# A second output buffer for the experts of a hybrid encoder layer, and one load buffer fewer

## The chip, the cores and the metric

The kernel runs on one core of one Trainium2 chip. The metric is the time of one execution on the device in microseconds (us), as the median of several runs. The engines are named as in the profile: PE (TensorE matmul), PEld (its weight loads), DVE (VectorE), ACT (ScalarE), POOL (GpSimd) and SP (SyncE). SP only issues transfers here; POOL issues the transfers that need an index per row.

## The reference

One layer of an encoder for 512 tokens of 1024 values, in float32. A first part (differential attention beside a gated linear recurrence, merged and projected) is not touched by the change. The last part is a mixture of experts:

```python
h2 = rms_norm(x, norm2_gain)
# router: one group of 4 by softmax and argmax, then 2 of its 4 experts; weights cs
a = einsum('nd,edf->nef', h2, w_gate)       # 16 experts, 1024 -> 512
u = einsum('nd,edf->nef', h2, w_up)
hid = silu(a) * u * cs[:, :, None]
y = einsum('nef,efd->nd', hid, w_down)      # 512 -> 1024, summed over the experts
x = x + y
```

Each token uses 2 of the 16 experts.

## The kernel before

The layer is computed in stages; the last one, from about 610 us on, is the experts' (lines 961 to 1094). The experts run one after the other. An expert has 104 slots for tokens. Its tokens are fetched by row index from DRAM (the "gather", L882) into one of two places of the buffer `hy`, transposed on PE (`xgp`) and split into exact high and low parts (`hx`). The products with the gate, up and down weights are each done as three PE passes (L1027 to L1029) over the weights' high and low parts.

The weights come in 12 loads of 512 KB for each expert (four of gate, four of up, four of down), 192 in all. Each load lands in one of 33 buffers that are used in turn (the list `raws`, with names such as `mr`, `raw`, `u0`, `h2`); a buffer comes free when ACT has copied its load to the high part (L171, `we_h` or `wd_h`) and DVE has formed the low part (L172, `we_l` or `wd_l`). All but three loads are issued by SP in one fixed order (L974); loads number 31 to 33, the first into the buffers `h2`, `h2` and `g2`, are issued by POOL (L972). The high and low parts have four buffers each.

The order of the program in one turn of the loop (expert e) is: gate product of e; in its middle the transposes of the hidden values of e - 1 (`hpt`, L1001); down product of e - 1 into two PSUM tiles `py`, with the transposes of the tokens of e + 1 and the slot search of e + 3 between its four loads; then the output of e - 1: two ACT copies of `py` (104x512 each, L1058) into a place of `hy`, and one transfer that adds the 104 rows to `out` in DRAM by index (the "scatter", L886, issued by POOL); then the up product of e. The framework orders instructions on each engine once, when the kernel is built, by an estimate of their readiness. So ACT, POOL and SP each work through a fixed list, and an instruction that waits holds up everything behind it on its engine.

The output has one place, `place(hy, 1, 0)`. The copies of expert e write where the scatter of expert e - 1 reads, so the first copy waits until that scatter has landed. Below, copy n, scatter n and gather n are those of expert n, counted from 0; gather n + 4 stands in POOL's list next to scatter n.

```python
add_out(ids[e][0].ix, py, place(hy, 1, 0)[0:CAP])     # end of down(e), L1053

def add_out(ix, py, y):
    for n in range(2):
        ACT.copy(y[:, n * 512:(n + 1) * 512], py[n])
    scatter_add(ix, y)
```

Of the kernel before, what the change touches and what calls it, by code (L numbers as in the profile page):

```python
# [10 lines left out]
F32 = mybir.dt.float32  # L11
# [8 lines left out]
P = 128  # L20
D = 1024
S = 512
# [11 lines left out]
RAW1 = 9  # L34
# [4 lines left out]
BEHIND = 30  # L39
# [7 lines left out]
# columns of the per-partition parameter block  # L47
# [7 lines left out]
# columns of the row parameters that every partition needs  # L55
# [6 lines left out]
# columns of the constants  # L62
# [45 lines left out]
def hybrid_layer(ctx, tc, x, w_in, w_ao, w_lo, w_out, w_lg, w_rt, w_eg, w_eu, w_ed, pp, rw, cst, out):  # L108
# [45 lines left out]
    # places of 4 KB, with one use after the other: tag -> (pool, number)  # L154
# [19 lines left out]
    def load_split(src, name, behind=()):  # L174
        # one chunk [128, 8, 256] of dense weights, in two halves of its rows
        hs, ls_ = [], []
        for i in range(2):
            t = wraw.tile([P, 1024], F32, tag="raw", name=f"{name}_r{i}")
            nc.sync.dma_start(t, src[:, i * 1024:(i + 1) * 1024])
            hi = wspl.tile([P, 1024], F32R, tag="whi", name=f"{name}_h{i}")  # L180
            lo = wspl.tile([P, 1024], F32R, tag="wlo", name=f"{name}_l{i}")
            with ExitStack() as order:
                for ins in behind[i:i + 1]:
                    order.enter_context(tc.issue_after(ins))
                split(hi, lo, t)
            hs += [hi[:, q * 256:(q + 1) * 256] for q in range(4)]
            ls_ += [lo[:, q * 256:(q + 1) * 256] for q in range(4)]
        return hs, ls_

    def mm3(ps, wh, wl, ah, al, first=True, last=True):  # L190
        # stationary (wh, wl), moving (ah, al)
        mm(ps, wh, ah, start=first, stop=False)  # L192
        mm(ps, wh, al, start=False, stop=False)  # L193
        return mm(ps, wl, ah, start=False, stop=last)

# [36 lines left out]
    # softplus(-lam) = max(-lam, 0) + log1p(exp(-|lam|)); log1p(z) = 2 atanh(z / (2 + z))  # L232
# [23 lines left out]
    # lambda of the differential attention, on every partition  # L256
# [9 lines left out]
    # rotary tables with the gains (k's carry sqrt(64))  # L266
# [20 lines left out]
    held = []          # what waits for results of the tensor engine, with how much of its next work goes before it  # L287
# [4 lines left out]
    def go_on(last, n):  # L292
        # n columns have passed up to here
        for h in held:
            h[0] -= n
        due = [h for h in held if h[0] <= 0]
        for h in due:
            held.remove(h)
            with tc.issue_after(last.ins):
                h[1]()  # L300
# [16 lines left out]
    gat = tc.alloc_tile_pool(name="gat", bufs=1)  # L317
    gT = gat.tile([P, KD, S], F32, name="gT")          # tanh of the lru gate, then the gated lru branch
# [7 lines left out]
    yG = [yp.tile([P, 2, S], F32, tag=f"y{j}", name=f"yG{j}") for j in range(4)]      # gelu(lru_gate)  # L326
    yT = [[None] * 4, [None] * 4]                                                     # the branch's output takes its place
    lp = tc.alloc_tile_pool(name="lru", bufs=1, side="right", reuse_waits="tile")
    xpt = [lp.tile([P, S + 3], F32, name=f"xp{i}") for i in range(2)]      # with the convolution's margins
# [5 lines left out]
    def gate_pieces(i, dst):  # L335
        # columns of gate_attn (i < 4) or gate_lru
        w = []

        def piece(cb):
            if cb == 0:  # L340
                w.extend(load_split(w_in[20 + i], f"wg{i}"))
            j = 2 * i + cb
            ps = pj(f"gps{j}")
            proj_T(ps, w, cb, h_)
            ACT.activation(dst[:, j % 8], ps, AF.Tanh, bias=hb[:, 32 + j:33 + j], scale=0.5)

        return [lambda: piece(0), lambda: piece(1)]
# [111 lines left out]
    def qk_half(pr, qi, tp):  # L459
        # half of the tokens of q (k) of two heads: projected and rotated; sums of squares for its norm  # L460
# [44 lines left out]
    def stack(pr, hh, qi):  # L505
        # transposed, then exact parts on top of each other: q as [hi; lo], k as [hi; lo] and [lo; hi]
        # (of the head's second map the other way round)
        j = pr.j
        ps = pm(f"tps{qi}{j}{hh}")
        for t in range(NT):  # L510
            PE.transpose(ps[:, t * P:(t + 1) * P], pr.qr[qi][:, t, hh * P:(hh + 1) * P], ident)
        names = ("q",) if qi == 0 else ("k0", "k1")
        st = [unit(n, [P, 2, S], F32R, f"st_{n}{j}{hh}") for n in names]
        for s in range(2):
            own, oth = slice(64 * s, 64 * s + 64), slice(64 - 64 * s, 128 - 64 * s)
            a = st[0][:, s]
            ACT.copy(a[own], ps[own])
            DVE.tensor_tensor(a[oth], ps[own], f(a[own]), op=ALU.subtract)
            pr.st[hh, qi, s, 0] = a
            if qi:  # L520
                b = st[1][:, s]
                ACT.copy(b[oth], ps[own])
                DVE.tensor_copy(b[own], a[oth])
                pr.st[hh, qi, s, 1] = b
# [24 lines left out]
    def apply_v(pr, hh, t, mx, ee):  # L549
        # e0 - lam (s0 / s1) e1, times v: the head's output times s0  # L550
# [50 lines left out]
    def new_o(h):  # L601
        # exact parts of a head's output, where the last heads' operands have left room
        o = unit(("qr", "qr", "va", "vb", "q", "k0", "k1", "ee")[h], [P, 2, S], F32R, f"o{h}")
        oS[h] = o[:, 0], o[:, 1]
        return oS[h]
# [8 lines left out]
    # lru branch projected and gated: gT <- (1 + tanh) * lru_d; the first two heads beside it  # L614
# [8 lines left out]
    # for the second norm and the router: the gains carry sqrt(D); the router takes x2 itself, the gain in its weights  # L623
# [25 lines left out]
    # what runs beside each step of a pair of heads: projections of the next pair, operands, gates  # L649
# [50 lines left out]
    places["sq"] = mraw1, 1  # L700
    x2 = [unit(tag, [P, D], F32, f"x2_{tag}") for tag in ("u0", "u1", "u2", "rope")]
# [23 lines left out]
    # of each token and expert, for its slot: valid, token in two parts, zero, weight and 1 / rms in three parts  # L725
# [4 lines left out]
    def post(t, part, c0, c1, then, eng=None):  # L730
        # of some columns: sum of squares, and the router's products with x2 turned
# [22 lines left out]
    def scaled(eng, t, c0, c1):  # L754
        # part of the normed tokens but for 1 / rms; written in two halves of the columns
        i = t // 2, c0 // 512
        if c0 % 512 == 0 and t % 2 == 0:
            h2[i] = unit("h2", [P, 2, 512], F32, f"h2_{t}{c0}")
        half = h2[i][:, t % 2]
        i_ = eng.tensor_tensor(half[:, c0 % 512:(c1 - 1) % 512 + 1], x2[t][:, c0:c1], g2r[:, c0:c1], op=ALU.mult)  # L760
        if c1 % 512 == 0:
            nc.sync.dma_start(h2d[t * P:(t + 1) * P, c1 - 512:c1], half)
        return i_.ins
# [22 lines left out]
    # group and experts of each token; its places within the experts, from 1; 0 where not chosen  # L786
# [3 lines left out]
    def route(t):  # L790
        # how many of the groups (of the group's experts) go before each one: larger, or equal and of a lower index
# [14 lines left out]
        # the tokens before those of the next block; the last time, all of them  # L806
# [8 lines left out]
    class Slots:  # L815
        # token (or a spare row), weight and 1 / rms of each slot of expert e, ranks CAP r ...
# [22 lines left out]
        def ids(self):  # L839
            # id = p + 128 t + (1 - valid) * slot  # L840
# [48 lines left out]
    # the tokens and their outputs lie where the merged branches were  # L889
# [7 lines left out]
    ids = {}  # L897

# [18 lines left out]
    # combine weights (with 1 / rms of the token), as exact bf16 parts  # L917
# [79 lines left out]
    def turn(name, src, k0, dst):  # L997
        # four blocks of 128 columns, transposed: [CAP, 4, 128] -> [128, 4, CAP], copied or split
# [26 lines left out]
    def mm3_(ps, ah, al, wh, wl, first, last):  # L1025
        # stationary (ah, al), moving (wh, wl)
        mm(ps, ah, wh, start=first, stop=False)  # L1027
        mm(ps, ah, wl, start=False, stop=False)  # L1028
        mm(ps, al, wh, start=False, stop=last)  # L1029
# [10 lines left out]
    def down(e, ht, between):  # L1040
# [12 lines left out]
        add_out(ids[e][0].ix, py, place(hy, 1, 0)[0:CAP])  # L1053
# [145 lines left out]
```

## Time and profile before

| | |
|---|---|
| median of 3 timed runs | 934.54 us (934.34 to 935.6) |
| profiled execution, first to last instruction (span) | 937.4 us |
| PE busy | 881.9 us, 94% of the span |
| DVE / ACT / POOL busy | 699.8 / 588.3 / 212.4 us |
| moved by the transfer engines | 169.99 MB, mean 181 GB/s |

The page gives no other time of the profiled execution than its span, which is 2.9 us above the median of the timed runs; differences are therefore worked out within the profiled execution and taken off the median. An engine's busy share is an average over the stages, so each stage is read from its own stretch of time.

### The profile page before, as it was taken

The numbers are of one execution on the slowest core, as the hardware profiler recorded it, in microseconds if no ns is written. First come the engines' busy times: TensorE is split into PE (matmuls) and PEld (weight loads), VectorE is DVE, ScalarE is ACT, GpSimd is POOL, SyncE is SP. The second block draws the span as 40 slices with busy tenths as digits, with TensorE's granted clock in tenths as the row PEclk, the third lists the DMA queues.
The fourth block names the chain that finished last, engine by engine and source line by source line (L and its number), as shares of the span: only waits on it lengthen the run. The fifth ranks groups of instructions, "written<-read, shape, count | busy, mean of one in ns | idle before, by whom it ended". The sixth has DMA issues, their size and how long they took to land. (4 is left out here: it accounts for less than half of the span.)

```text
span 937.4 us, 13453 instructions
## 1 busy us (share of the span) xinstructions
PE 881.9 (94%) x4950; PEld 729.2 (78%) x4950; DVE 699.8 (75%) x1077; ACT 588.3 (63%) x917; POOL 212.4 (23%) x183
## 2 busy tenths in 40 slices
PE   4999999999999999999999999877999999999993
PEld 3887787889999889999888899855676777777772
DVE  4548978854488688896895643676897999999992
ACT  6698796622364664664785323345786888888881
POOL 6500000053026026053110003331442131121010
PEclk9999999999999999999999999978999999999998
DMA  6421312232212112112226286689999999999922
GB/s 229 171 72 63 138 68 91 96 133 90 90 62 75 50 58 71 49 46 68 105 98 234 103 296 227 218 296 259 334 375 334 375 375 355 349 377 352 376 60 36
DMA packets 48061, 169.99 MB, mean 181 GB/s; under 512 B 6177, under 2 KB 6225, under 8 KB 47985
## 3 DMA queue, kind: packets, MB, share of 16 engines
q1 hardware_dynamic: 41040, 147.34, 43.3%
q0 software_dynamic: 6944, 21.68, 9.0%
q8 instruction: 41, 0.67, 0.3%
q14 instruction: 36, 0.29, 0.1%
HBM read 156.94 MB, written 12.06 MB: 180 GB/s over the span
## 5 line engine op out<-in xcount | busy, mean ns | idle before, releaser
L172 DVE TENSOR_TENSOR we_l<-we,we_h 128x1024 fp32r<-128x1024 f32 x128 | 153.8, 1224 | 21.7 <-ACT we_h L171 19.8
L171 ACT CAST we_h<-we 128x1024 fp32r<-128x1024 f32 x128 | 132.1, 1051 | 25.7 <-PE mgu L1029 14.1
L1027 PE MATMUL mgu<-we_h,hx 128*104 128x512 f32 x256 | 103.6, 405 | 3.1 <-ACT we_h L171 2.5
L1028 PE MATMUL mgu<-we_l,hx 128*104 128x512 f32 x256 | 103.1, 403 | 1.7 <-DVE we_l L172 1.6
L1029 PE MATMUL mgu<-we_h,hx 128*104 128x512 f32 x256 | 102.5, 400 | 0.0
L171 ACT CAST wd_h<-wd 128x1024 fp32r<-128x1024 f32 x64 | 67.3, 1051 | 24.1 <-PE mgu L1029 24.1
L167 POOL TENSOR_TENSOR rk<-ss,mhalf 128x8 f32<-128x8 f32 x16 | 26.4, 1648 | 245.6 <-DVE ss L474 245.6
L172 DVE TENSOR_TENSOR wd_l<-wd,wd_h 128x1024 fp32r<-128x1024 f32 x64 | 77.6, 1222 | 5.8 <-ACT wd_h L171 5.7
L886 POOL DMA_INDIRECT out_dram<-hy,ix x16 | 33.4, 2090 | 191.8 <-DVE ix L844 112.6
L312 PE MATMUL qps<-wqk_l,hT 128*128 128x256 f32 x256 | 72.4, 283 | 1.2 <-DVE wqk_l L172 1.2
L311 PE MATMUL qps<-wqk_h,hT 128*128 128x256 f32 x256 | 73.4, 287 | 0.0
L313 PE MATMUL qps<-wqk_h,hT 128*128 128x256 f32 x256 | 72.5, 283 | 0.0
L1027 PEld LDWEIGHTS mgu<-we_h,hx 128*104 128x104 f32 x256 | 44.0, 172 | 19.8 <-ACT we_h L171 3.4
L1028 PEld LDWEIGHTS mgu<-we_l,hx 128*104 128x104 f32 x256 | 44.0, 172 | 18.3 <-DVE we_l L172 2.7
L1029 PEld LDWEIGHTS mgu<-we_h,hx 128*104 128x104 f32 x256 | 44.1, 172 | 16.0
L545 ACT ACTIVATE ee<-sps,mx 128x512 f32<-128x512 f32 x64 | 43.9, 691 | 17.1 <-DVE mx L544 17.0
L544 DVE TENSOR_REDUCE mx<-sps 128x1 f32<-128x512 f32 x64 | 42.6, 682 | 16.1 <-PE sps L542 15.9
L1027 PE MATMUL py<-wd_h,hh 128*104 128x512 f32 x128 | 52.5, 414 | 0.6 <-ACT hh L171 0.6
L192 PE MATMUL gps<-hT,wg_h 128*128 128x512 f32 x128 | 50.8, 397 | 0.0
L1029 PE MATMUL py<-wd_h,hl 128*104 128x512 f32 x128 | 50.4, 395 | 0.0
L1028 PE MATMUL py<-wd_l,hh 128*104 128x512 f32 x128 | 50.3, 393 | 0.0
L193 PE MATMUL gps<-hT,wg_h 128*128 128x512 f32 x128 | 50.3, 393 | 0.0
(307 smaller groups left out, 2535.0 us busy)
## 6 DMA issues: line engine op xcount, KB each, us to landing
wd<-in_w_ed_dram SPq DMA_DIRECT2D x64, 512.0 KB, 12.4
we<-in_w_eg_dram SPq DMA_DIRECT2D x63, 512.0 KB, 12.9
we<-in_w_eu_dram SPq DMA_DIRECT2D x62, 512.0 KB, 11.6
wg_r<-in_w_in_dram SPq DMA_DIRECT2D x16, 512.0 KB, 3.6
wqk_r<-in_w_in_dram SPq DMA_DIRECT2D x16, 512.0 KB, 3.6
wy_r<-in_w_in_dram SPq DMA_DIRECT2D x8, 512.0 KB, 5.5
wx_r<-in_w_in_dram SPq DMA_DIRECT2D x8, 512.0 KB
wlo_r<-in_w_lo_dram SPq DMA_DIRECT2D x8, 512.0 KB, 4.1
```

What stands on the lines that cost most here:

```text
L171: ACT.copy(dst_hi, src)
L172: eng.tensor_tensor(dst_lo, src, f(dst_hi), op=ALU.subtract)
L192: mm(ps, wh, ah, start=first, stop=False)
L193: mm(ps, wh, al, start=False, stop=False)
L311: mm(ps, a, w[0][k], start=(k == 0), stop=False)
L312: mm(ps, a, w[1][k], start=False, stop=False)
L313: last = mm(ps, b, w[0][k], start=False, stop=(k == KD - 1))
L544: DVE.tensor_reduce(mx[:, c:c + 1], ps, axis=AX.X, op=ALU.max, negate=True)
L545: ACT.activation(ee[:, c], ps, AF.Exp, bias=mx[:, c:c + 1], accum_out=(pr.s0s[hh][:, t:t + 1] if c == 0 else mx[:, 3:4]))
L1027: mm(ps, ah, wh, start=first, stop=False)
L1028: mm(ps, ah, wl, start=False, stop=False)
L1029: mm(ps, al, wh, start=False, stop=last)
```

## The change

A new buffer `y2` of [128, 1024] float32 is allocated in the pool in which the load buffers named `mr` lie. The copies and the scatter of experts with an odd number use `y2`, those with an even number use the place in `hy` as before. To make room, the buffers named `mr` are five instead of six (`RAW1 - 3`), so that the list `raws` has 32 entries instead of 33, and `BEHIND` goes from 30 to 29, so that the last three loads of the first round (now number 30 to 32, again into `h2`, `h2` and `g2`) are still the ones that POOL issues. The new file also has no comments, and its lines stand one lower from line 700 on and two lower from line 900 on.

```diff
-RAW1 = 9
+RAW1 = 8
...
-BEHIND = 30
+BEHIND = 29
...
     places["mr"] = mraw1, RAW1 - 3
     places["h2"] = mraw1, 2
     places["sq"] = mraw1, 1
+    places["y2"] = mraw1, 1
...
     ids = {}
+    y2 = unit("y2", [P, D], F32, "y2")
...
-        add_out(ids[e][0].ix, py, place(hy, 1, 0)[0:CAP])
+        add_out(ids[e][0].ix, py, (y2 if e % 2 else place(hy, 1, 0))[0:CAP])
```

ACT's list around the output of expert 1, before. A name in brackets is a semaphore that the instruction waits for; DMASW ones tell of the landing of a transfer that POOL issued, DMAHW ones of one that SP issued. Copy 1 is the first row with `COPY`.

```order
L171 CAST we_h<-we_6570 128x1024 [waits DMASW4_49,DVE_49,PE_49]
L1058 COPY hy<-py_6465 104x512 [waits DMASW2_49,PE_49]
L1058 COPY hy<-py_6466 104x512 [waits PE_49]
L171 CAST we_h<-we_6582 128x1024 [waits DMASW5_49,DVE_49]
L171 CAST we_h<-we_6599 128x1024 [waits DVE_49,DMASW6_49,PE_49,Activation_49]
```

The same place of ACT's list now:

```order
L171 CAST we_h<-we_6571 128x1024 [waits DMASW5_49,DVE_49,PE_49]
L1060 COPY y_5989<-py_6466 104x512 [waits PE_49]
L1060 COPY y_5989<-py_6467 104x512 [waits PE_49]
L171 CAST we_h<-we_6583 128x1024 [waits DMASW6_49,DVE_49]
L171 CAST we_h<-we_6600 128x1024 [waits DVE_49,PE_49,Activation_49]
```

The order is the same; copy 1 no longer waits for DMASW2, which scatter 0 raises.

POOL's list there now (L883 is a gather, L887 a scatter; ix0 to ix7 are the experts' indices). It has the same order as before, with `hy_5988` in place of `y2_5989`:

```order
L883 DMA hy_5988<-h2d_238,ix4_0_6334 104x1024 [waits DMASW7_49,DVE_49,PE_49]
L887 DMA out_0_dram<-hy_5988,ix0_0_5982 640x1024 [waits DMASW3_49,Activation_49]
L887 DMA out_0_dram<-y2_5989,ix1_0_5999 640x1024 [waits DMASW2_49,Activation_49]
L883 DMA hy_5988<-h2d_238,ix5_0_6523 104x1024 [waits DMASW0_49,DMASW4_49,DVE_49,PE_49]
L883 DMA hy_5988<-h2d_238,ix6_0_6712 104x1024 [waits DMASW1_49,DMASW5_49,DVE_49,PE_49]
L887 DMA out_0_dram<-hy_5988,ix2_0_6072 640x1024 [waits DMASW6_49,DMASW3_49,Activation_49]
L887 DMA out_0_dram<-y2_5989,ix3_0_6190 640x1024 [waits DMASW6_49,Activation_49]
```

What each scatter waits for is unchanged: scatter 1 still waits for DMASW2, the landing of scatter 0. SP's list is the old one with each load of the experts one buffer further on.

## Rows read from the trace of the kernel before

**Rows 1.** Busy time by stretch: PE, PEld, DVE, ACT, POOL, granted clock, DMA share, GB/s.

```profile
740.00:760.00 20.00, 20.00 (x100) 14.81 (x99) 19.19 (x22) 16.88 (x21) 3.63 (x2) 1.00 1.03 360
```

**Rows 2.** Waits of PE, 640 us on: total, times, longest (us).

```profile
PE mgu L1027 <- ACT we_h L171: 2.5, 2, 1.3
PE mgu L1028 <- DVE we_l L172: 1.6, 2, 0.8
```

**Rows 3.** Timeline of PE (start, length, idle before, releaser): the first waits.

```profile
676.38 0.47 PE L1027 MATMUL mgu<-we_h,hx 128*104 128x512 f32 x1 [1.13 <-ACT we_h L171]
...
715.03 0.47 PE L1027 MATMUL mgu<-we_h,hx 128*104 128x512 f32 x1 [1.34 <-ACT we_h L171]
```

**Rows 4.** Timeline of ACT: copies 1, 2 and 3.

```profile
674.31 1.07 ACT L1058 COPY hy<-py 104x512 f32<-104x512 f32 x2 [3.75 <-DMA out_dram<-hy,ix]
...
690.87 1.26 ACT L1058 COPY hy<-py 104x512 f32<-104x512 f32 x2
...
712.96 1.07 ACT L1058 COPY hy<-py 104x512 f32<-104x512 f32 x2 [3.98 <-DMA out_dram<-hy,ix]
```

**Rows 5.** Waits of ACT, 640 us on.

```profile
ACT hy L1058 <- DMA out_dram<-hy,ix: 7.7, 2, 4.0
```

**Rows 6.** Timeline of POOL, 653 to 718 us: scatters L886, gathers L882.

```profile
659.98 4.44 POOL L886 DMA_INDIRECT out_dram<-hy,ix  x1 [0.30 <-ACT we_h L171]
675.69 1.62 POOL L886 DMA_INDIRECT out_dram<-hy,ix  x1 [11.27 <-ACT hy L1058]
677.62 2.00 POOL L882 DMA_INDIRECT hy<-h2d,ix  x1 [0.30 <-DVE we_l L172]
693.27 6.21 POOL L882 DMA_INDIRECT hy<-h2d,ix  x1 [13.65 <-PE mgu L1029]
699.78 4.40 POOL L886 DMA_INDIRECT out_dram<-hy,ix  x1 [0.30 <-ACT wd_h L171]
714.34 1.62 POOL L886 DMA_INDIRECT out_dram<-hy,ix  x1 [10.16 <-ACT hy L1058]
```

**Rows 7.** Timeline of PE: hpt of experts 1 to 5; xgp of expert 5.

```profile
661.32 0.52 PE L1001 MATMUL hpt<-cst_sb,hy 104*128 104x104 f32 x4
...
681.66 0.52 PE L1001 MATMUL hpt<-cst_sb,hy 104*128 104x104 f32 x4
...
699.65 0.52 PE L1001 MATMUL hpt<-cst_sb,hy 104*128 104x104 f32 x4
...
704.24 0.52 PE L1001 MATMUL xgp<-cst_sb,hy 104*128 104x104 f32 x4
...
721.87 0.52 PE L1001 MATMUL hpt<-cst_sb,hy 104*128 104x104 f32 x4
...
739.83 0.52 PE L1001 MATMUL hpt<-cst_sb,hy 104*128 104x104 f32 x4
```

**Rows 8.** Busy time by stretch, around the second wait of PE.

```profile
716.90:720.30 3.40, 3.40 (x10) 2.31 (x9) 3.40 (x5) 1.96 (x2) 1.36 (x1) 0.50 1.05 364
720.30:730.00 9.70, 9.70 (x53) 7.24 (x52) 8.73 (x9) 8.00 (x10) 0.00 (x0) 1.00 1.03 352
```

**Rows 9.** Transfer issues: queue, count, KB each, median us to landing.

```profile
wd<-in_w_ed_dram SPq DMA_DIRECT2D x64, 512.0 KB, 12.4
...
hy<-h2d,ix POOLq DMA_INDIRECT x16, 11.2
```

**Rows 10.** Timeline of SP: issues of four loads each.

```profile
649.65 6.13 SPq L974 DMA_DIRECT2D wd<-in_w_ed_dram  x4
...
879.68 6.48 SPq L974 DMA_DIRECT2D wd<-in_w_ed_dram  x4
```

**Rows 11.** Timeline of ACT: the cast of the last load.

```profile
915.56 1.05 ACT L171 CAST wd_h<-wd 128x1024 fp32r<-128x1024 f32 x1 [0.31 <-PE mgu L1029]
```

**Rows 12.** Busy time by stretch: where loads wait for buffers, and the last full one.

```profile
650.00:656.00 6.00, 5.91 (x29) 4.07 (x28) 4.40 (x7) 4.96 (x7) 2.04 (x1) 1.00 0.63 227
...
880.00:890.00 10.00, 10.00 (x53) 7.44 (x51) 9.37 (x10) 8.22 (x11) 0.00 (x0) 1.00 1.03 372
```

## The prediction

> **What bounds the kernel now.** I read the stage of the experts first by its busy time per stretch. In a full stretch of 20 us PE is busy for all 20, DVE for 19.19 and ACT for 16.88, and the transfer engines' share is 1.03 [rows 1]. So PE sets the pace, and the loads run at the engines' limit beside it. The view of waits, from 640 us to the end, says how often PE is held up there: twice by a high part from ACT, 2.5 us in all, and twice by a low part from DVE, 1.6 us in all [rows 2]; two waits further on, in the last expert, come after the last load was cast and are not touched. PE's timeline puts the two pairs at 676 and at 715 us [rows 3].
>
> Going back one step, ACT's timeline shows what held the high parts up. Copy 1 begins at 674.31 after ACT stood idle for 3.75 us, and copy 3 at 712.96 after 3.98 us, both released by the landing of a scatter; copy 2, between them, did not wait [rows 4]. These two are all the time that copies lost to scatters, 7.7 us in 2 waits [rows 5]. Back one more step, POOL's timeline: scatter 0 starts only at 659.98, right behind a gather, and takes 4.44 us to issue; scatter 2 starts at 699.78, behind a gather of 6.21 us, and takes 4.40 us; scatters 1 and 3 take 1.62 us each [rows 6]. From their starts to the release of the copies, scatter 0 needs 674.31 - 659.98 = 14.3 us and scatter 2 needs 712.96 - 699.78 = 13.2 us. So the single place for the outputs binds at two experts of sixteen, where the scatter started late.
>
> **What the two waits cost.** What an expert takes without a wait is read from the distance of the transposes hpt: from expert 2 to 3 it is 699.65 - 681.66 = 17.99 us, and from 4 to 5 it is 739.83 - 721.87 = 17.96 us; I take 17.98. From 1 to 2 it is 681.66 - 661.32 = 20.34 us, and from 3 to 4 it is 721.87 - 699.65 = 22.22 us [rows 7]. The waits therefore cost 2.36 and 4.24 us. Of the second, 3.40 us passed at a granted clock of 0.50 (1.2 instead of 2.4 GHz) after PE had stood still, from 716.90 on; at full clock the same work takes half, so 1.70 us are the clock's [rows 8]. The rest is PE's idle time, (2.5 + 1.6) = 4.1 us in both places [rows 2], and some 0.8 us of slow start.
>
> **What the change removes.** Copy 1 writes `y2`, which nobody has read yet, and in ACT's list it has no wait for a transfer left. Copy 2 waits for scatter 0, copy 3 for scatter 1, and so on: one turn more. With PE 2.36 us ahead, copy 2 comes at 690.87 - 2.36 = 688.5 [rows 4], and scatter 0 landed at 674.3, 14 us before. Scatter 1 can start when scatter 0 has landed, at 674.3, and by the slowest of the two landings, 14.3 us, it is through at 688.6; copy 3 comes at 712.96 - 3.98 - 2.36 = 706.6, 18 us after. Both waits of ACT go, with nothing in their place on ACT: 2.36 + 4.24 = 6.60 us.
>
> **What the change adds.** No instruction: the same 32 copies and 16 scatters, of the same shapes. Two costs remain to be bounded.
>
> First, POOL. Scatter 1 still waits for scatter 0, and what is queued behind it is gather 5, then gather 6. Gather 5 started at 677.62 [rows 6]; now it starts behind scatter 1 at about 674.3 + 1.62 + 0.3 = 676.2. It lands a median of 11.2 us later [rows 9], at 687.4, and PE wants it for the transposes xgp of expert 5, which stood at 704.24 [rows 7] and come 2.36 us earlier: 14 us of cover. In the same way scatter 3 waits for scatter 2, which lands 13.2 us after its start at 699.78 - 2.36, so at 710.6; gather 7 follows at about 712.5 and lands at 724, and expert 7's transposes come a whole turn after 721.87 - 6.60. The cost is 0; without the cover PE would wait for the gather as it would for any operand, by what exceeds those 14 us.
>
> Second, the ring of 32 buffers. A load now waits until the next load in the order has been consumed, one step longer. That matters where the loads already wait for buffers: from 650 to 656 us the transfer share is only 0.63 [rows 12], and four loads were issued over 6.13 us, so (6.13 - 0.33) / 3 = 1.93 us apart, the 0.33 being one issue [rows 10]. There everything lands about 1.9 us later, and since the engines are full from then on (share 1.03 up to 890 us [rows 1, 12]) it stays so. What hides it is the lead of the loads: the last is issued at 879.68 + 6.48 = 886.2 at the latest [rows 10], lands by the median of 12.4 us [rows 9] at 898.6, and is cast at 915.56 [rows 11], so the lead is 17.0 us. It falls to 17.0 - 6.6 - 1.9 = 8.5 us and stays positive. Cost 0; if the cover were gone, PE would lose what is missing from it.
>
> The sum: 0 - 6.60 + 0 + 0 = -6.60 us. In the profiled execution this is 937.4 - 6.6 = 930.8 us of span; I take the same difference off the median of the timed runs, 934.54 - 6.60 = 927.94, because the waits' causes (an order and its durations) are no different there. The unknown is how much of the loss PE gets back. At the least it is the idle time alone, 4.1 us (930.4): ACT and DVE could stay as close behind as they are now, and the clock could fall elsewhere. At the most it is all that ACT lost, 7.7 us [rows 5], and the clock's 1.70, so 9.4 us (925.1). I take the distances between the transposes, since they measure PE's own loss whole.
>
> Of the clock, the Trainium skill (TensorE: Matmul & The Clock Gate, Part 1) says that how many slow matmuls a kernel meets varies from run to run of the same kernel. The trace has one execution, so no run here shows that yet; by that rule the 1.70 us would be missing in some runs before, and the gain there would be 4.90 us.
>
> **The rivals.** *A part only comes back:* PE gains the idle time and no more, 4.1 us, 930.4. For it: the clock at 0.50 is seen after one of the two waits only, so it need not be bound to them. Against it: the distances 17.99 and 17.96 on either side show what a turn without a wait takes.
>
> *The wait moves to POOL:* the scatters still go one at a time, so POOL stands where ACT stood, and the gathers behind are late. It decides once a gather loses its 14 us of cover, so with landings of 28 us instead of 14; if the gathers of experts 5 and 7 were late by what was won, 2.36 and 4.24, the time would stay at 934.5. For it: POOL's list, in which scatter 1 waits for DMASW2 as before. Against it: the landings are 14.3 and 13.2 us, under the 17.98 of a turn, so the chain of scatters does not fall behind.
> The Trainium skill (DMA: Bandwidth & Descriptors, Rules for kernel authors) speaks for this rival: a transfer that accumulates must wait for an earlier one to the same bytes, since a write in between is lost. By that rule a second buffer never puts two scatters in flight, and what it frees is ACT alone; the order of the new kernel agrees.
>
> *The shorter ring starves PE (slower):* if the loads, with 32 buffers, kept waiting for buffers as between 650 and 656 us, they would come 1.93 us apart, while PE uses one each 17.98 / 12 = 1.50 us. The lead would shrink by 0.43 us per load; the 8.5 us that are left are gone after 20 loads, the 6.6 us gained after 15 more. Over 50 loads, four experts, PE would lose 50 x 0.43 - 8.5 = 13.0 us, and the time would be 934.54 - 6.60 + 13.0 = 940.9. For it: one stretch with the share at 0.63, and a buffer less. Against it: the share is full in every later stretch that I read, and buffers come free earlier once PE no longer stands.
>
> *It does not do what it says:* the even copies could still be held because `hy` also holds tokens and hidden values. The order excludes it for copy 1, and copy 2 did not wait before either; I give it no chance of its own beyond the second rival's.
>
> **How the numbers follow.** The forecast, both waits gone, has 0.76 (927.9; its own range 925.1 to 930.4); a part only 0.11 (930.4); moved to POOL 0.08 (934.5); starved 0.05 (940.9). A measurement of this kernel tells 0.2%, 1.9 us, from no change. The first two cases are faster: 0.87, of which I leave 0.01 to a gain under 1.9 us; same 0.09; slower 0.05, so faster 0.86. The range takes the forecast's own bounds and 1 us beyond the partial case for the lead that I only know by a median: 925.0 to 931.5.
>
> **What would show it.** Right: in the profile after, no copy released by a scatter; PE's waits for high and low parts gone between 660 and 730 us; all distances of hpt from expert 1 to 12 near 17.98; the granted clock 1.00 through 700 to 730 us; the last load's cast still well after its landing. POOL should show scatters 1 and 3 waiting for the scatters before them, with no wait of PE for tokens. Wrong: distances over 18.5 us with a copy or a gather as releaser (second rival), or PE behind high parts that wait for loads (third). A gain under 4 us with all waits gone would mean that the distances measured something else than these waits.

## The result and the profile after

Over 16 runs each, the changed kernel has a median of 930.53 us (927.79 to 933.28) and the kernel before one of 935.93 us (932.88 to 939.75). The ratio is 0.9933, with a 95% interval of 0.9921 to 0.9946. Of 935.93 us that is 6.3 us less, between 5.1 and 7.4; the medians alone differ by 5.4 us. The forecast was 6.60 us less, and 927.9 us in all; the time came out 2.6 us higher, 1.4 us of which is the median of before, which stood at 934.54 us in the three runs shown then.

The waits of PE from 640 us on (total, times, longest, in us) are now these. The pairs of [rows 2] are gone; the two that are left belong to the last expert and were there before.

```profile
PE hpt L1003 <- DVE hy L1039: 0.8, 1, 0.8
PE py L1029 <- ACT hh L171: 0.6, 1, 0.6
```

ACT's timeline of the changed kernel (start, length in us), copies 1, 2 and 3, which answer to [rows 4]. None has an idle time and a releaser in brackets behind it any more.

```profile
668.40 1.25 ACT L1060 COPY y<-py 104x512 f32<-104x512 f32 x2
...
686.39 1.27 ACT L1060 COPY hy<-py 104x512 f32<-104x512 f32 x2
...
704.35 1.25 ACT L1060 COPY y<-py 104x512 f32<-104x512 f32 x2
```

PE's timeline, the transposes hpt of experts 0 to 5 and of 15:

```profile
633.72 0.52 PE L1003 MATMUL hpt<-cst_sb,hy 104*128 104x104 f32 x4
...
659.25 0.52 PE L1003 MATMUL hpt<-cst_sb,hy 104*128 104x104 f32 x4
...
677.19 0.52 PE L1003 MATMUL hpt<-cst_sb,hy 104*128 104x104 f32 x4
...
695.18 0.52 PE L1003 MATMUL hpt<-cst_sb,hy 104*128 104x104 f32 x4
...
713.14 0.52 PE L1003 MATMUL hpt<-cst_sb,hy 104*128 104x104 f32 x4
...
731.13 0.52 PE L1003 MATMUL hpt<-cst_sb,hy 104*128 104x104 f32 x4
...
907.70 0.58 PE L1003 MATMUL hpt<-cst_sb,hy 104*128 104x104 f32 x4 [0.84 <-DVE hy L1039]
```

And the same of before for experts 0 and 15; expert 1's is in [rows 7].

```profile
634.31 0.52 PE L1001 MATMUL hpt<-cst_sb,hy 104*128 104x104 f32 x4
...
916.36 0.57 PE L1001 MATMUL hpt<-cst_sb,hy 104*128 104x104 f32 x4 [0.84 <-DVE hy L1037]
```

From expert 1 to 15 it took 916.36 - 661.32 = 255.04 us before, and takes 907.70 - 659.25 = 248.45 us now: 6.59 us less. Up to expert 12 every turn (from one hpt to the next) now takes 17.94 to 18.00 us; before, two took 20.34 and 22.22. The last three turns are shorter in both kernels (17.76, 17.74 and 15.23 us now). This distance is used below for every kernel ("1 to 15"), because it leaves out what happens ahead of expert 1.

That stretch ahead matters for one reading. The profiled span fell by 937.4 - 928.9 = 8.5 us, more than the 6.59. Most of the rest, 27.01 - 25.53 = 1.48 us, lies between expert 0 and 1. Busy time by stretch, of before and then of after (the columns as in [rows 1]; the last but two is the granted clock):

```profile
638.40:641.80 3.40, 2.25 (x10) 2.03 (x11) 0.99 (x2) 1.01 (x2) 0.00 (x0) 0.50 1.03 317
641.80:645.20 3.40, 3.40 (x9) 2.32 (x8) 0.74 (x1) 1.04 (x1) 0.00 (x0) 0.50 1.05 236
```

```profile
638.40:641.80 3.40, 3.12 (x13) 2.62 (x14) 0.59 (x1) 1.01 (x2) 0.00 (x0) 0.50 1.05 289
641.80:645.20 3.40, 3.40 (x16) 2.52 (x15) 1.85 (x3) 2.10 (x2) 0.00 (x0) 1.00 1.00 264
```

The clock stood at 0.50 in both halves before and in the first half only after. A second profile of the changed kernel (after2, below) has 0.50 and 0.54 there, and 27.08 us from expert 0 to 1. So this part varies between executions of one kernel, and the change has no claim on it.

POOL's timeline after, from gather 4 on, answers to [rows 6]:

```profile
651.90 5.72 POOL L883 DMA_INDIRECT hy<-h2d,ix  x1 [15.57 <-DVE ix L845]
657.93 4.44 POOL L887 DMA_INDIRECT out_dram<-hy,ix  x1 [0.30 <-ACT we_h L171]
672.74 1.74 POOL L887 DMA_INDIRECT out_dram<-y,ix  x1 [10.38 <-DMA out_dram<-hy,ix]
674.79 4.87 POOL L883 DMA_INDIRECT hy<-h2d,ix  x1 [0.30 <-DVE M L832]
688.12 5.05 POOL L883 DMA_INDIRECT hy<-h2d,ix  x1 [8.45 <-issue]
693.48 1.63 POOL L887 DMA_INDIRECT out_dram<-hy,ix  x1 [0.30 <-issue]
706.23 1.70 POOL L887 DMA_INDIRECT out_dram<-y,ix  x1 [11.13 <-DVE ix L845]
```

Scatter 1 now waits on POOL for scatter 0. But something changed that the prediction had not foreseen: gather 6 and scatter 2 take 5.05 + 1.63 = 6.7 us to issue, where they took 6.21 + 4.40 = 10.6 us. So scatter 2 is out early, and scatter 3 needs no wait for it.

### The profile page after: what moved, and what is told of

Read it like the earlier page. It is cut to its first block, busy times and chain, and to the rows that moved or that the text cites. A ratio compares the mean times of both kernels' runs of the same rounds, so it can differ in the third digit from the quotient of the medians.

```text
span 928.9 us, 13453 instructions
## 1 busy us (share of the span) xinstructions
PE 877.0 (94%) x4950; PEld 727.0 (78%) x4950; DVE 700.1 (75%) x1077; ACT 588.5 (63%) x917; POOL 210.3 (23%) x183
## 4 chain that ended last, share of the span: by engine, by line
PE 69%; DVE 15%; ACT 8%; DMA 4%; issue 2%; POOL 0%; SPq 0%; POOLq 0%; ACTq 0%
PE mgu L1030 6%; PE mgu L1029 6%; PE mgu L1031 6%; PE py L1029 3%; PE py L1031 3%; PE py L1030 3%; PE ops L565 3%; PE qps L312 2%; PE qps L313 2%; PE qps L311 2%; DMA hy<-h2d,ix 2%; PE aps L192 2%; PE aps L194 2%; PE lps L194 2%; PE aps L193 2%
## 5 line engine op out<-in xcount | busy, mean ns | idle before, releaser
L312 PEld LDWEIGHTS qps<-wqk_l,hT 128*128 128x128 f32 x256 | 48.7, 190 | 2.0 <-DVE wqk_l L172 1.6
```

The source lines that it names most:

```text
L312: mm(ps, a, w[1][k], start=False, stop=False)
```

## The experiments

| kernel | output places | load buffers | ratio to before, 95% interval | 1 to 15, us |
|---|---|---|---|---|
| before | 1 | 33 | | 255.04 |
| changed | 2 | 32 | 0.9933 [0.9921, 0.9946] | 248.45 |
| after2 (the changed one again) | 2 | 32 | 0.9946 [0.9928, 0.9964] | 248.41 |
| ring32 | 1 | 32 | 0.9999 [0.9985, 1.0013] | 255.10 |
| ring28 | 2 | 28 | 0.9947 [0.9928, 0.9966] | 248.42 |
| only1 | 2, the second for expert 1 alone | 32 | 0.9922 [0.9905, 0.9939] | 248.33 |
| only3 | 2, the second for expert 3 alone | 32 | 0.9959 [0.9943, 0.9974] | 251.69 |
| scfirst | 1, scatters 0 and 2 ahead of gathers 4 and 6 | 33 | 0.9919 [0.9898, 0.9941] | 248.43 |
| scfirst1 | 1, written for scatter 0 only | 33 | 0.9942 [0.9923, 0.9962] | 248.48 |
| both | 2, and scatters first | 32 | 0.9935 [0.9915, 0.9956] | 248.43 |
| gaps | 1, DVE's run broken everywhere | 33 | 0.9925 [0.9898, 0.9952] | 248.92 |
| gapswd | 1, broken at the down weights only | 33 | 0.9980 [0.9963, 0.9997] | 252.45 |
| aftergaps | 2, broken everywhere | 32 | 0.9919 [0.9893, 0.9946] | 248.90 |

**The ring.** ring32 is before with the shorter ring alone; ring28 is the changed kernel with four buffers fewer.

```diff
-RAW1 = 9          # before -> ring32
+RAW1 = 8          # ring28: 4
-BEHIND = 30
+BEHIND = 29       # ring28: 25
```

> The ring of 32 load buffers alone; the outputs keep their one place. Theory (all of the gain comes from the copies that no longer wait for a scatter; the shorter ring costs nothing): no change against the kernel before, within 1 us; in the profile copies 1 and 3 wait for a scatter some 3.8 and 4.0 us as before, and the distances of hpt are about 20.3 (expert 1 to 2) and 22.2 us (3 to 4), 18.0 elsewhere. Rival (the other order of the loads brings part of the gain, seen as 2 us less before the transposes hpt of expert 1): 1.5 to 2 us faster. Rival (a shorter ring starves PE): slower.

> Two output places, with a ring of 28 load buffers instead of 32 (four of the buffers named mr fewer). Theory (the ring only eats the lead of the loads over their casts, 1.5 us for each buffer, and the lead of the last load in the changed kernel is about 11 us): the lead falls by 4 x 1.5 = 6 us and stays positive, so the time is that of the changed kernel within 0.2%, 0.9930 of before. Rival (the ring is at its limit with 32 and the loads starve PE soon): distances of hpt over 18.5 us with waits for high parts whose loads landed late, and 5 us or more lost against the changed kernel.

Both came out as the theory had it. ring32 has before's time, its 7.7 us of waits of copies in two places and its two long turns (20.27 and 22.26 us). ring28 has the changed kernel's time (0.9947 beside 0.9946 for after2, in one series). How near the ring is to its limit is read from the lead of the last load, by the prediction's own recipe (end of the last issue, plus the median landing, up to the cast). The issues by SP, the summary of issues and ACT's cast, first of the changed kernel, then of ring28:

```profile
880.22 4.13 SPq L976 DMA_DIRECT2D wd<-in_w_ed_dram  x4
...
wd<-in_w_ed_dram SPq DMA_DIRECT2D x64, 512.0 KB, 12.0
...
906.90 1.05 ACT L171 CAST wd_h<-wd 128x1024 fp32r<-128x1024 f32 x1 [0.31 <-PE mgu L1031]
```

```profile
884.23 4.16 SPq L976 DMA_DIRECT2D wd<-in_w_ed_dram  x4
...
wd<-in_w_ed_dram SPq DMA_DIRECT2D x61, 512.0 KB, 13.2
...
905.76 1.05 ACT L171 CAST wd_h<-wd 128x1024 fp32r<-128x1024 f32 x1 [0.30 <-PE mgu L1031]
```

The leads are 906.90 - 884.35 - 12.0 = 10.6 us, and 905.76 - 888.39 - 13.2 = 4.2 us: four buffers cost 6.4 us of lead, 1.6 us each. The recipe itself is good to about 1 us only, since it goes by a median: for after2, the same kernel as the changed one, it gives 908.71 - 886.85 - 12.4 = 9.5 us, and so 1.3 us for each buffer. At these rates the rest would last for two or three buffers more; that wasn't run.

**Which copy needs the second place.** Everything is as in the changed kernel but for the choice of the place.

```diff
-        add_out(ids[e][0].ix, py, (y2 if e % 2 else place(hy, 1, 0))[0:CAP])
+        add_out(ids[e][0].ix, py, (y2 if e == 1 else place(hy, 1, 0))[0:CAP])    # only3: e == 3
```

> Ring of 32, and only expert 1 uses the second output buffer. Theory: copy 1 does not wait, copy 3 still waits for scatter 2; the distance of hpt from expert 1 to 2 is 18.0 us, from 3 to 4 above 20; faster than before by about 2.4 us. Rival (the two waits are one lag that is handed on, so that taking away the first only makes the second longer): no gain, with copy 3 waiting 6 us or more.

> Ring of 32, and only expert 3 uses the second output buffer. Theory: copy 1 waits 3.8 us as before, copy 3 does not wait; distances of hpt 20.3 (1 to 2) and 18.0 us (3 to 4); faster than before by about 4.2 us, of which 1.7 us from the granted clock that no longer falls near 717 us. Rival (the clock falls anyway somewhere near): 2.5 us.

only3 agrees in time: 0.41% of 937.78 us, the median of before in that series, is 3.8 us (2.4 to 5.3). Its distances do not. By "1 to 15" it gains 3.35 us, and the turn from expert 1 to 2, with the one wait that is left, takes 21.92 us instead of the 20.3 expected. PE's timeline of only3 (hpt of experts 1 and 2), and its busy time in a stretch of that turn, with the granted clock as the last column but two:

```profile
660.78 0.52 PE L1003 MATMUL hpt<-cst_sb,hy 104*128 104x104 f32 x4
...
682.70 0.52 PE L1003 MATMUL hpt<-cst_sb,hy 104*128 104x104 f32 x4
```

```profile
678.10:681.50 3.40, 3.40 (x9) 2.33 (x8) 3.40 (x5) 1.70 (x3) 1.00 (x1) 0.50 1.04 334
```

In before the clock stood at 1.00 there. So the clock's loss did not go with the second wait, as the theory had it; it moved to the first. gapswd, below, in which the first wait alone is left too, shows the same: 22.00 us from expert 1 to 2, and a clock of 0.50 from 675.2 to 678.6 us. Between 645 and 915 us the four profiles with such waits of PE (before, ring32, only3, gapswd) have one stretch at 0.50 each, behind the last of them, and the nine without have none. Why the first wait alone draws it, and not when a second follows, is not shown. The other turns of only3 up to expert 12 take 17.92 us instead of 17.97, which nothing here explains and which makes up 0.6 of its 3.35 us; the rest, 2.7 us, is near the rival's 2.5 (the clock falls anyway).

only1 misses the expectation further: it brings the whole gain where 2.4 us were expected. Its copy 3 waits for scatter 2 in the same place of `hy` as before, and yet for 0.90 us only, which PE doesn't feel. ACT's and POOL's timelines of only1 show why:

```profile
707.01 1.07 ACT L1060 COPY hy<-py 104x512 f32<-104x512 f32 x2 [0.90 <-DMA out_dram<-hy,ix]
```

```profile
689.83 5.05 POOL L883 DMA_INDIRECT hy<-h2d,ix  x1 [8.37 <-issue]
695.18 1.63 POOL L887 DMA_INDIRECT out_dram<-hy,ix  x1 [0.30 <-issue]
```

As in the changed kernel, scatter 2 is out sooner in its turn: at 696.81, 0.07 us ahead of the hpt of expert 3 (696.88), where before it was out 4.53 us behind it (704.18 and 699.65 [rows 6, 7]). So the two waits were no two independent costs. Nor is the second simply the echo of the first: in only3 copy 1 still waits, 3.78 us, and there too gather 6 and scatter 2 take 5.07 and 1.63 us. gapswd, below, has one place, and there copy 1 waits, 3.80 us, and copy 3 does not.

**The order of scatter and gather.** One place and 33 buffers as before, but gathers 4 and 6, with their slot searches, are issued behind scatters 0 and 2 instead of ahead of them.

```diff
-        if e + 3 < N_EXP:
+        if e + 3 < N_EXP and e not in FIRST:            # FIRST = (1, 3); scfirst1: (1,)
             todo = todo + [lambda: tokens(e + 3)]
         if e:
-            down(e - 1, hid[e - 1], dict(enumerate([p_] for p_ in todo)))
+            sc = down(e - 1, hid[e - 1], dict(enumerate([p_] for p_ in todo)))
+            if e in FIRST:
+                tokens(e + 3, sc)                       # the gather is issued after scatter sc
```

> One output place and the ring of 33, as before; instead gathers 4 and 6, with their slot searches, are written behind scatters 0 and 2, so that POOL issues the scatter first. Theory (the copies wait because scatters 0 and 2 start 6 us late behind a gather): scatter 0 starts near 654 instead of 660 us and scatter 2 about 6 us earlier than before, no copy waits, all distances of hpt near 18.0 from expert 1 on, and the gain is that of the second buffer, 6 to 7 us. Rival (a scatter takes 13 to 14 us to land because the transfer engines are full, whenever it starts): copies 1 and 3 still wait, 0 to 2 us each, and the gain is 3 to 5 us. Rival (the gathers are late now): PE waits for tokens, slower.

> One output place and 33 load buffers as before; only gather 4 is issued behind scatter 0 instead of ahead of it, gather 6 stays where it was. Theory (the second wait is a consequence of the first: with PE not held at expert 1, POOL's gather 6 and scatter 2 are issued at another moment, take some 3.5 us less together, and scatter 2 lands before copy 3): the whole gain, 0.992 to 0.994 of before, all distances of hpt from expert 2 on near 17.98, copy 3 waits under 1.5 us. Rival (the two waits are independent, as the sum of the prediction has them): only the first one's 2.4 us come back, 0.9975, and the distance from expert 3 to 4 stays near 22.2.

> The changed kernel (two output places, 32 load buffers), and gathers 4 and 6 issued behind scatters 0 and 2. Theory (either edit alone already removes all that the single place costs): nothing more than either, 0.992 to 0.994 of before, distances of hpt near 17.98. Rival (the scatters' order holds something else as well): another 2 us or more off.

scfirst gains as much as the change does, without a second place. POOL's timeline of it:

```profile
651.44 2.23 POOL L887 DMA_INDIRECT out_dram<-hy,ix  x1 [14.92 <-ACT hy L1063]
653.98 3.69 POOL L883 DMA_INDIRECT hy<-h2d,ix  x1 [0.31 <-issue]
...
687.52 1.61 POOL L887 DMA_INDIRECT out_dram<-hy,ix  x1 [13.86 <-DVE we_l L173]
```

Scatter 0 starts right behind its copy, and copy 1 finds the place free. What the single place cost was thus the late start of two scatters. scfirst1 gave the whole gain too, but it doesn't decide whether the second wait hangs on the first: in its POOL timeline scatter 2 stands ahead of gather 6 (687.60 and 689.87 us) as in scfirst, because the framework's order moved along. "both" adds nothing to either edit.

**What makes an issue on POOL long.** Three kernels break DVE's run of subtractions by a tiny instruction on an unused tile.

```diff
     def split_e(t, name, eng=DVE):
...
         split(hi, lo, t, eng)
+        DVE.memset(gap1, 0.0)          # gap1: [1, 8]; gapswd: only if name starts with "wd"
         return hi, lo
```

> The kernel before (one output place, 33 load buffers), and after each low part of the experts' weights DVE also sets 8 elements of an unused tile to zero, so that its big subtractions no longer follow each other directly. Question: what sets the 1.6 to 6.2 us that an indirect transfer of POOL takes to issue. Theory (it waits for DVE to pause from subtractions of two operands in SBUF, which follow each other directly 3 to 5 times): gathers and scatters take at most some 2.5 us each, scatter 0 starts earlier by 3 us or more, the copies wait less than half of the 7.7 us, and the time lies at 0.993 to 0.997 of before if DVE has the room. Rival (the length is POOL's own or the transfer queue's): gather 4 still takes 5 to 6 us and scatter 0 4 to 5 us, and the time is that of before or up to 0.3% above it for DVE's 190 small instructions.

> The kernel before, with the small instruction only after the low parts of the down weights (64 of the 192); between the low parts of the gate and up weights, over which gathers 4 and 6 are issued, nothing stands. Theory (what counts is whether DVE's run of subtractions is broken where POOL issues): gather 4 takes 5.5 to 6 us and gather 6 5 to 6.3 us as before, scatter 0 starts as late as before, copy 1 waits 3 us or more, and the time is at most 0.3% from before. Rival (the small instructions help in some other way, through DVE's pace or the loads): gathers 4 and 6 under 3 us, or a gain of 0.5% with the gathers as long as before.

> The changed kernel (two output places, 32 load buffers) with the small instruction after every low part of the experts' weights. Theory (with the waits of ACT gone nothing is left for shorter issues to win, and PE sets the pace): 0.992 to 0.995 of before, as either alone. Rival (shorter issues win something besides): below 0.990.

First the kernel before. Its DVE timeline, where POOL issues gather 4, and POOL's row:

```profile
653.07 5.76 DVE L172 TENSOR_TENSOR we_l<-we,we_h 128x1024 fp32r<-128x1024 f32 x5
658.75 0.73 DVE L1037 SCALAR_TENSOR_TENSOR hy<-hy,svt,mgu 104x512 f32<-104x512 f32 x1
```

```profile
653.96 5.72 POOL L882 DMA_INDIRECT hy<-h2d,ix  x1 [17.04 <-DVE ix L844]
```

The gather begins inside a run of five subtractions, which end at 658.83, and is done at 659.68, 0.85 us after that. (The DVE instruction behind the run has an operand in PSUM.) Scatter 0 then starts inside the next run. Now gaps, the same place in the turn, DVE's timeline and POOL's:

```profile
648.26 1.21 DVE L172 TENSOR_TENSOR we_l<-we,we_h 128x1024 fp32r<-128x1024 f32 x1
648.27 0.07 DVE L992 MEMSET gap<- 1x8 f32 x1
649.40 1.22 DVE L172 TENSOR_TENSOR we_l<-we,we_h 128x1024 fp32r<-128x1024 f32 x1
649.41 0.07 DVE L992 MEMSET gap<- 1x8 f32 x1
```

```profile
649.13 1.19 POOL L882 DMA_INDIRECT hy<-h2d,ix  x1 [11.68 <-DVE gap L992]
650.63 2.67 POOL L886 DMA_INDIRECT out_dram<-hy,ix  x1 [0.31 <-issue]
...
685.26 1.18 POOL L882 DMA_INDIRECT hy<-h2d,ix  x1 [14.13 <-issue]
686.74 2.61 POOL L886 DMA_INDIRECT out_dram<-hy,ix  x1 [0.30 <-issue]
```

With an instruction of 0.07 us after each subtraction, gather 4 takes 1.19 instead of 5.72 us and scatter 0 takes 2.67 instead of 4.44. The gather, done at 650.32, again ends 0.85 us after a subtraction (649.47), but it is the one in which it began. No copy waits, and the whole gain is there with one place. The ratio, 0.9925, lies just below the range expected (0.993 to 0.997), and its interval reaches into the range. The 192 instructions seem to cost a little: here and in aftergaps the turns take 17.92 and 18.17 us by turns, 0.07 us more on average than 17.97.

gapswd is the control. As the theory had it, gather 4, over a run without a break, again takes 5.72 us, scatter 0 4.44, and copy 1 waits 3.80 us. Gather 6 missed the expectation, with 1.16 us instead of 5 or more. DVE's and POOL's timelines there:

```profile
690.58 1.22 DVE L172 TENSOR_TENSOR we_l<-we,we_h 128x1024 fp32r<-128x1024 f32 x1
692.09 3.56 DVE L172 TENSOR_TENSOR we_l<-we,we_h 128x1024 fp32r<-128x1024 f32 x3 [0.29 <-ACT we_h L171]
```

```profile
691.51 1.16 POOL L882 DMA_INDIRECT hy<-h2d,ix  x1 [14.46 <-issue]
692.97 1.85 POOL L886 DMA_INDIRECT out_dram<-hy,ix  x1 [0.30 <-issue]
```

DVE had to wait 0.29 us for a high part just then, and the gather was through at 692.67, 0.87 us after the subtraction that ended before the pause (691.80). It is the theory's own condition, a break in the run, that came from elsewhere. The changed kernel has a smaller one. DVE's timeline, the run of four over which gather 6 is issued, of before and then of after:

```profile
693.98 4.62 DVE L172 TENSOR_TENSOR we_l<-we,we_h 128x1024 fp32r<-128x1024 f32 x4
```

```profile
688.82 4.73 DVE L172 TENSOR_TENSOR we_l<-we,we_h 128x1024 fp32r<-128x1024 f32 x4
```

Before, the gather was done at 699.48, 0.88 us after the run's end (698.60). After, the run took 0.11 us longer, so it had a short pause inside, and the gather was done at 693.17, before the run's end (693.55). That the pause let it through is the likely reading; no run changes it alone. So when scatter 2 is out turns on some tenths of a microsecond between POOL and DVE. Of the profiles with gather 6 ahead of scatter 2, before and ring32 alone show 4.40 us for that scatter; in the others it is 1.6 to 2.6.

An unbroken run does not always hold an issue to its end, though. Gather 7 of before, in DVE's and POOL's timelines:

```profile
715.00 4.63 DVE L172 TENSOR_TENSOR we_l<-we,we_h 128x1024 fp32r<-128x1024 f32 x4 [4.04 <-ACT we_h L171]
```

```profile
716.27 2.00 POOL L882 DMA_INDIRECT hy<-h2d,ix  x1 [0.30 <-issue]
```

It began inside a run of four and was done at 718.27, while the run went on to 719.63; gather 5 (677.62, 2.00 us [rows 6]) did the same in a run of three that lasted from 676.36 to 679.86. What let these two in is not shown.

aftergaps, with both cures, has the gain of either: PE has no wait left that they could take away. Its median, 928.23 us against 936.54 us for before in that series, is the lowest of those here, but the interval doesn't part it from the changed kernel.

## Why the prediction was right, step by step

- *Both waits of ACT go, and nothing takes their place on ACT:* right; no copy has a transfer as releaser.
- *The sum, 6.60 us, from the distances of hpt:* right in size; the same distances give 6.59 us, and the timed runs 5.1 to 7.4. ring32 repeats the two long turns (20.27 and 22.26 us), so the loss was not the chance of one execution, and its total does not hang on how it is split. The lower bound, the idle time of 4.1 us alone, is excluded by that first series; the series of after2 by itself (0.9946, so 3.4 to 6.7 us) would not exclude it.
- *2.36 and 4.24 us as two costs of the single place:* this is the step that failed, though the sum hides it. The first term alone was to bring 2.4 us and brought everything (only1); the second alone was to bring 4.2 and brought 3.8 by time and 3.35 by the distances (only3), where the first wait then cost 21.92 - 17.92 = 4.0 us; together they make more than there is. The second wait needs a late scatter 2, and with gather 6 ahead of it scatter 2 was late only where gather 6 was held to the end of DVE's run of four and scatter 2 then met the next run (before and ring32). [Rows 6] had the sign of it, issue lengths of 1.62 to 6.21 us for the same kinds of instruction, and the prediction took them as given.
- *The clock's 1.70 us:* right that the stretch at 0.50 near 717 us goes with the waits; the stretch from 716.90 to 720.30 now has 1.00. Wrong that it belongs to the second: with the first wait alone left it came behind that one (only3, gapswd). For the sum this makes no difference, since the change takes both waits away. The rule of the Trainium skill (TensorE: Matmul & The Clock Gate, Part 1) that the number of slow matmuls varies between runs of one kernel is now shown by two profiles of the changed kernel, 25.53 and 27.08 us from expert 0 to 1, but at another place than the one priced.
- *POOL's cost 0:* right. The wait did move there: POOL's idle time ahead of scatter 1, 10.38 us, now ends with the landing of scatter 0, where it ended with copy 1 before (11.27 us [rows 6]). That is as the second rival and the Trainium skill (DMA: Bandwidth & Descriptors, Rules for kernel authors) have it. But it stays without a price, since PE waits for no tokens from 640 us on. That scatter 3 would wait for scatter 2 until 710.6 us was wrong: it started at 706.23.
- *The shorter ring costs 0:* right, by ring32. Its working was too dear: the lead was to fall to 17.0 - 6.6 - 1.9 = 8.5 us and is 10.6 (9.5 in after2). ring32, where the ring alone is shorter, has 913.14 - 885.09 - 12.0 = 16.1 us instead of 17.0, so one buffer fewer took about 0.9 us of lead where 1.9 was reckoned, as far as a recipe good to 1 us can tell.

## What to carry to other kernels

Two stalls in a row should not be added up as two costs of one cause before it is known what makes each of them late: ask for each one why its releaser started when it did, and do not tie the clock's loss to one of them. A buffer that binds at two turns of sixteen may point, as here, to a late start of what frees it, and then the order of two instructions on one queue, or a break in another engine's work, does what a second buffer does. A ring's length is judged by the lead of its last load; here five buffers fewer cost no time.

## What the runs showed of the hardware

An indirect transfer takes POOL 1.2 to 6.2 us to issue in the experts' stage, and a run of DVE's subtractions of two operands in SBUF can hold it up: gather 4 took 5.72 us over a run of five and 1.19 us with 0.07 us of another instruction after each subtraction (before, gaps), and gather 6 took 1.16 us with a pause of 0.29 us (gapswd). In these cases, and for gather 6 of before, it is done 0.85 to 0.88 us after the end of a subtraction that no other followed directly. This is not the whole rule, since gathers 5 and 7 of before took 2.00 us and were done before the end of the unbroken runs in which they began. The Trainium skill (SBUF — State Buffer, Who interferes with whom) says that a DVE instruction with two inputs in SBUF contends with a GpSimd instruction that reads SBUF, and that one blocks the other for the whole instruction; by that an issue that reads its indices in SBUF would lose, as an estimate, the rest of one subtraction, at most 1.22 us. Gathers 5 and 7 agree with that; gathers 4 and 6 of before, held over five and four subtractions, lost more. The same section reports that `tensor_tensor` did not stall a DMA in its probe; in the runs here, with indirect transfers, it did. That the ports are the cause is the page's account; the runs show only the relation in time.

The granted clock fell to 0.50 behind the last wait of PE in each of the four profiles that have such waits, whichever wait that was, and in none of the nine others (between 645 and 915 us); behind the first wait it cost some 1.6 to 1.7 us, by the turns from expert 1 to 2 of 21.92 and 22.00 us (only3, gapswd) beside 20.34 and 20.27 (before, ring32).
